# A third pair of k-tiles with seven products in the key and value blocks of a cross-attention

## The chip, the cores and the metric

The kernel runs on one core of a Trainium2 chip. The metric is device time in microseconds (us) of one execution, taken as the median over several runs; lower is better. The engines are named as the profile names them: PE is TensorE's matmuls, PEld its weight loads, DVE is VectorE, ACT is ScalarE, POOL is GpSimd, and SP issues the transfers (DMAs).

## The reference

One layer of a streaming encoder, 256 tokens of 2048 channels, in f32. Each part adds to the residual x: half a SwiGLU feed-forward, a mixer (pooling beside gated linear attention), a cross-attention to 256 memory tokens, and half a second SwiGLU; a final norm ends it. The part that the change touches is this one:

```python
def mem_cross_attention(h, mem_h, w_q, w_kv, w_o):
    q = (h @ w_q).reshape(b, s, XATTN_HEADS, XATTN_HEAD_DIM)
    kv = (mem_h @ w_kv).reshape(b, mem_h.shape[1], 2, XATTN_HEADS, XATTN_HEAD_DIM)
    k, v = kv[:, :, 0], kv[:, :, 1]
    logits = jnp.einsum('bshd,bmhd->bhsm', q, k).astype(jnp.float32) * (XATTN_HEAD_DIM ** -0.5)
    p = jax.nn.softmax(logits, axis=-1).astype(v.dtype)
    o = jnp.einsum('bhsm,bmhd->bshd', p, v).reshape(b, s, D_MODEL)
    return o @ w_o
```

There are 4 heads of 512 channels. `mem_h @ w_kv` is a product of 256 x 2048 by 2048 x 4096.

## The kernel before

**Products in three parts.** TensorE works on a format that holds fewer bits than f32, so every operand is kept as a high part (a rounded copy, written by ScalarE) and a low part (what is left, written by VectorE). A product is three matmuls: high by high, activation high by weight low, activation low by weight high (`products`, line 351). `xs` holds the activations of the current part, 16 k-tiles of 128 channels, and `ys` those of the next.

**Units and blocks.** Weights come in units of 1 MB: two k-tiles (a pair, numbered 0 to 7) by 1024 columns. A block of columns is `block_s` (line 487): eight units, taken in the order of pairs that the caller gives. Each unit is computed in one of two ways.
- Whole (`unit_p`): 2 k-tiles x 2 halves of the tokens x 2 halves of the columns, 8 products, 24 matmuls, all on line 356. Its weights are split into `wh` (ScalarE, line 273) and `wl` (VectorE, line 274).
- Seven (`unit_s` and `seven`, line 480): a Strassen-Winograd scheme, 7 products P1 to P7 on sums of operands, 21 matmuls. Its weights need three sums into a tile `T` (VectorE, line 457, three instructions), the split of the raw quarters into `xh` and `xl` (lines 273 and 274), and that of the sums into `wh` and `wl` (lines 460 and 461). The activations need sums too, once for each pair and for all blocks that share them (`Sums.make`, lines 418 to 430, and the splits of lines 279 and 280), kept in the tile `ye`. P1, P2, P3 use `xh` and `xl`; P7, P5, P6, P4 use `wh` and `wl`.

**Accumulators.** PSUM holds four tiles of two banks. A block keeps two of them from its first unit on for the sums P2, P4 and P3 and the whole products; from its first unit of seven on (`open_parts`) it keeps two more, for P1 and P6 and for P7 and P5, until `combine` (lines 547 to 552: one copy on ScalarE, three sums on VectorE) has read them behind the last unit of seven. Two joins (line 562) end the block. Everything else that TensorE writes (transposes, logits, values) takes tiles out of the same four.

**Order of the work.** `Stream` (line 34) lists units and, between them, operations that come due after a given number of units. The loads run three units ahead of the splits, on the SP queue, and the splits two units ahead of the matmuls. Within these bounds a planner of the framework sets the order of the instructions on each engine when the program is built; each engine then works in that order, and waits where it must.

**The stage.** The query product runs first (two blocks). Then come four blocks, with `xs` holding the memory tokens: keys of heads 0 and 1, values of heads 0 and 1, keys of heads 2 and 3, values of heads 2 and 3 (lines 1348 to 1359). Behind a block of keys, its result is transposed (`turn_K`, line 752), due one unit into the following block of values, the logits of both heads are due after two units (`logits`, line 1291, which also holds the softmax, lines 1297 to 1307), and the transposes of the probabilities after three (`probs`, line 1313). Behind a block of values, `ev_V` splits V into high and low (lines 279 and 280), and `values` (line 1330) is due one unit into the next block. In this stage, `KV_HOMES` lends the tiles of the units of seven other buffers: `T` takes turns with the results of `combine` on two buffers "sg", and `xh` and `xl` share two buffers "att".

Before the change, pairs 0 and 4 are computed by seven products, in one order for all four blocks: 1, 5, 2, 0, 3, 6, 4, 7. So the units of seven stand at places 3 and 6, counted from 0.

## Time and profile before

| | |
|---|---|
| median of 3 runs | 2085.72 us (2085.29 to 2086.19) |
| span of the profiled execution | 2085.1 us |
| TensorE busy / weight loads / VectorE / ScalarE | 99% / 83% / 87% / 55% |
| granted TensorE clock, mean | 0.998 |
| the stretch from 1110 to 1328 us (the four blocks) | PE 218.0, PEld 184.7, DVE 168.6, ACT 106.6 us |

The page gives the span of the profiled execution, from its first to its last instruction; it gives no other time for that execution. The times of the runs lie 0.2 to 1.1 us above it.

A line of the order of time reads: start in us, length, engine, line, operation, out<-in, shapes, how many instructions the row merges; in brackets the idle time before it and what ended it. The chain is the work that ended last, followed back from the end, as start, length, engine, tile, line, count. A busy matmul is modelled 0.39 us long while the next one starts much earlier, so the cost of a matmul is read from start to start. Lines of code behind 1260 stand one line lower in the changed kernel.

### The profile page before, as it was taken

The page shows a single profiled execution, that of the slowest core. Times are in us where ns is not written, and L with a number is a line of the kernel's source. Part 1 is how long each engine was busy: PE and PEld are TensorE (multiplying, and loading weights), DVE is VectorE, ACT ScalarE, POOL GpSimd, SP SyncE. Part 2 cuts the span into 40 slices and gives each one's busy share as a digit, 9 for nine tenths or more (in the row PEclk, how much of TensorE's full clock was granted, in tenths as well). Part 3 has the DMA queues.
Part 4 walks back from the last instruction along what each step waited for, and adds up shares of the span by engine and source line. Part 5 has one row for each costly group of instructions (what it writes and reads, how often), then busy time and mean ns, then how long its engine had stood idle before and what let it go on. Part 6 is the DMA issues. An engine that isn't in the chain of part 4 may idle for free.

```text
span 2085.1 us, 24238 instructions
## 1 busy us (share of the span) xinstructions
PE 2071.5 (99%) x9660; PEld 1727.2 (83%) x9660; DVE 1820.8 (87%) x1670; ACT 1137.5 (55%) x1128; POOL 13.1 (1%) x41
## 2 busy tenths in 40 slices
PE   9999999999999999999999999999999999999998
PEld 7888888888888888888888888888888888888886
DVE  6999899989998677579789777879998999989997
ACT  7555455554555545455755444556554556545554
POOL 0000000000000000000000000000000000000001
PEclk9999999999999999999999999999999999999999
DMA  7656766566656755457655455666576665676664
GB/s 263 201 189 235 242 220 204 187 229 232 225 197 234 238 177 182 162 182 269 225 186 188 162 182 179 205 223 203 181 242 213 236 209 190 223 241 223 204 223 159
DMA packets 131321, 435.94 MB, mean 209 GB/s; under 512 B 9860, under 2 KB 13544, under 8 KB 130824
## 3 DMA queue, kind: packets, MB, share of 16 engines
q1 hardware_dynamic: 131176, 434.38, 61.4%
q8 instruction: 76, 1.25, 0.2%
q14 instruction: 37, 0.30, 0.0%
q10 hardware_dynamic: 32, 0.01, 0.0%
HBM read 417.58 MB, written 16.78 MB: 208 GB/s over the span
## 4 chain that ended last, share of the span: by engine, by line
PE 96%; DVE 2%; issue 1%; ACT 0%; DMA 0%; SPq 0%; DVEq 0%
PE pt L356 57%; PE pt L480 26%; PE pa L341 6%; PE pb L356 2%; PE ph L752 1%; PE pl L1291 1%; PE pv L1330 1%; PE px L763 1%; DVE wl L461 0%; DVE T L457 0%; DVE xl L274 0%; DVE wl L274 0%; DMA x<-in_x 0%; PE pp L984 0%; PE pe L356 0%
## 5 line engine op out<-in xcount | busy, mean ns | idle before, releaser
L274 DVE TENSOR_TENSOR wl<-raw,wh 128x2048 fp32r<-128x2048 f32 (+2 forms) x264 | 591.4, 2247 | 131.1 <-ACT wh L273 130.4
L356 PE MATMUL pt<-wh,xs 128*128 128x512 f32 x2128 | 681.8, 390 | 0.0
L273 ACT CAST wh<-raw 128x2048 fp32r<-128x2048 f32 (+2 forms) x264 | 495.4, 1880 | 284.4 <-PE pt L356 128.1
L356 PEld LDWEIGHTS pt<-wh,xs 128*128 128x128 f32 x2128 | 398.2, 188 | 81.7 <-ACT wh L273 0.4
L356 PE MATMUL pt<-wh,ys 128*128 128x512 f32 x1472 | 464.7, 390 | 0.0
L460 ACT CAST wh<-T 128x1024 fp32r<-128x1024 f32 x236 | 248.0, 1054 | 380.5 <-DVE T L457 370.0
L356 PE MATMUL pt<-wl,xs 128*128 128x512 f32 x1064 | 415.5, 391 | 0.0
L356 PEld LDWEIGHTS pt<-wh,ys 128*128 128x128 f32 x1472 | 275.9, 188 | 56.9
L356 PE MATMUL pt<-wl,ys 128*128 128x512 f32 x736 | 286.3, 389 | 0.0
L461 DVE TENSOR_TENSOR wl<-T,wh 128x2048 fp32r<-128x2048 f32 x118 | 269.5, 2284 | 0.7
L356 PEld LDWEIGHTS pt<-wl,xs 128*128 128x128 f32 x1064 | 199.8, 188 | 41.1
L274 DVE TENSOR_TENSOR xl<-raw,xh 128x1536 fp32r<-128x1536 f32 x118 | 206.7, 1752 | 19.2 <-ACT xh L273 19.2
L273 ACT CAST xh<-raw 128x1536 fp32r<-128x1536 f32 x118 | 174.6, 1480 | 41.4 <-PE pt L480 29.2
L457 DVE TENSOR_TENSOR T<-T,raw 128x512 f32<-128x512 f32 x236 | 162.8, 690 | 6.2
L356 PEld LDWEIGHTS pt<-wl,ys 128*128 128x128 f32 x736 | 138.2, 188 | 28.6
L457 DVE TENSOR_TENSOR T<-raw 128x1024 f32<-128x1024 f32 x118 | 143.8, 1219 | 0.5
L480 PE MATMUL pt<-wh,xs 128*128 128x512 f32 x364 | 141.8, 389 | 0.0
L480 PE MATMUL pt<-xh,xs 128*128 128x512 f32 x364 | 136.6, 391 | 0.1
L341 PE MATMUL pa<-xs,wh 128*128 128x512 f32 x384 | 135.6, 397 | 0.0
L480 PE MATMUL pt<-wh,xe 128*128 128x512 f32 x320 | 124.5, 389 | 0.0
L341 PE MATMUL pa<-xs,wl 128*128 128x256 f32 x384 | 106.8, 282 | 0.0
L341 PEld LDWEIGHTS pa<-xs,wh 128*128 128x128 f32 x384 | 71.7, 188 | 16.4 <-issue 0.3
(244 smaller groups left out, 2215.6 us busy)
## 6 DMA issues: line engine op xcount, KB each, us to landing
raw<-in_ffn_w_down SPq DMA_DIRECT2D x88, 1024.0 KB, 5.5
raw<-in_ffn_w_up SPq DMA_DIRECT2D x80, 1024.0 KB, 5.0
raw<-in_ffn_w_gate SPq DMA_DIRECT2D x77, 1024.0 KB, 5.1
raw<-in_w_in SPq DMA_DIRECT2D x32, 1024.0 KB, 5.2
raw<-in_xattn_w_kv SPq DMA_DIRECT2D x32, 1024.0 KB, 5.0
raw<-in_w_out SPq DMA_DIRECT2D x16, 1024.0 KB, 5.6
raw<-in_xattn_w_q SPq DMA_DIRECT2D x16, 1024.0 KB, 5.6
raw<-in_xattn_w_o SPq DMA_DIRECT2D x16, 1024.0 KB, 5.9
```

The source lines that it names most:

```text
L273: in_turn("scalar", lambda: nc.scalar.copy(hi, src))
L274: in_turn("vector", lambda: nc.vector.tensor_tensor(out=lo, in0=src, in1=f32(hi), op=ALU.subtract))
L341: nc.tensor.matmul(o, w, x, start=k == 0 and i == 0, stop=last and i == 1)
L356: nc.tensor.matmul(ps, a, w, start=first and i == 0, stop=last and i == 2)
L457: in_turn("vector", lambda: nc.vector.tensor_tensor(out=o, in0=a, in1=b, op=ALU.add))
L460: in_turn("scalar", lambda: nc.scalar.copy(th[:, c], t[:, c]))
L461: in_turn("vector", lambda: nc.vector.tensor_tensor(out=tl, in0=t, in1=f32(th), op=ALU.subtract))
L480: nc.tensor.matmul(banks[n], x, w, start=n in fresh and j == 0, stop=n in ends and j == 2)
L752: nc.tensor.transpose(v[:, i, h * P : (h + 1) * P], g[:, h, i * P : (i + 1) * P], ident)
L763: nc.tensor.transpose(v[:, j, h * P : (h + 1) * P], x[:, h, j * P : (j + 1) * P], ident)
L1291: nc.tensor.matmul(ps[:, t, :M], ys[:, 4 * h + d, a, tok], xa["K", h][:, d, b, :], start=i == 0, stop=i == 11,)
L1330: nc.tensor.matmul(ps[:, d, :S], xa["V", h][:, m, a, col], xa["PT", h][:, m, b, :], start=i == 0, stop=i == 5,)
```

## The change

A third pair, number 2, is computed by seven products in all four blocks. Its sums of activations are made in addition, due after the third unit, and `ye` holds three pairs instead of two. The order of the pairs changes: the first block of keys takes 1, 5, 3, 0, 6, 2, 4, 7 (seven at places 3, 5 and 6), and the other three blocks take 1, 2, 5, 0, 3, 4, 6, 7 (seven at places 1, 3 and 5).

```diff
-    kv_sums, KV_ORDER = Sums("ye", xs, (0, 4), True, 2), (1, 5, 2, 0, 3, 6, 4, 7)
+    kv_sums = Sums("ye", xs, (0, 2, 4), True, 3)
+    KV_ORDER = ((1, 5, 3, 0, 6, 2, 4, 7), (1, 2, 5, 0, 3, 4, 6, 7))
...
-    for g, after in zip(kv_sums.pairs, (0, 2)):
+    for g, after in zip(kv_sums.pairs, (0, 2, 3)):
         st.op(lambda g=g: among_weights(lambda: kv_sums.make(g)), after)
     for b in range(2):
-        block_s(wwide(w_kv, b * 2 * NB), xs, kv_sums, KV_ORDER, lambda j, c, b=b: held.__setitem__(
+        block_s(wwide(w_kv, b * 2 * NB), xs, kv_sums, KV_ORDER[b], lambda j, c, b=b: held.__setitem__(
             ("K", 2 * b + j), c))
...
-        block_s(wwide(w_kv, D + b * 2 * NB), xs, kv_sums, KV_ORDER, ev_V(b))
+        block_s(wwide(w_kv, D + b * 2 * NB), xs, kv_sums, KV_ORDER[1], ev_V(b))
```

## The prediction

> **What bounds the kernel now.** First the page: its first line, the busy line and the chain that ended last.

> ```profile
> span 2085.1 us, 24238 instructions
> PE 2071.5 (99%) x9660; PEld 1727.2 (83%) x9660; DVE 1820.8 (87%) x1670; ACT 1137.5 (55%) x1128; POOL 13.1 (1%) x41
> PE 96%; DVE 2%; issue 1%; ACT 0%; DMA 0%; SPq 0%; DVEq 0%
> ```

> The time is TensorE's, and VectorE stands right behind it. The second view is the stretches view of the four blocks of keys and values, which I call K1, V1, K2, V2 in the order in which they run. Its columns are PE, weight load, VectorE and ScalarE busy.

> ```profile
> 1110.00:1328.00 218.00, 218.00 (x1077) 184.68 (x1076) 168.55 (x155) 106.61 (x102) 0.00 (x0) 1.00 0.52 177
> ```

> TensorE never rests here, and VectorE has 49.5 us to spare, in pieces. Third, the chain in order of time (start, length, what):

> ```profile
> 1060.25 5.44 PE pt L356 x24
> 1065.69 0.47 PE pt L480 x2
> 1066.18 1.49 ACT xh L273
> 1067.70 1.77 DVE xl L274
> 1069.51 2.11 PE pt L480 x8
> 1117.33 10.43 PE pt L356 x46
> 1143.40 1.75 PE ph L752 x16
> 1153.69 5.63 PE pl L1291 x47
> 1163.67 0.44 PE pt L1313 x4
> ```

> 46 matmuls take 10.43 us, so a matmul costs 0.2267 us, start to start. A whole unit (24) is 5.44 us and a unit of seven products (21) is 4.76 us. The four rows from 1065.69 show what a wait ahead of a unit of seven looks like; it lies in the query block, ahead of the change.

> **The change, part by part.** *Products.* Each of the four blocks drops one of eight products of one pair: 3 matmuls, 12 in all, 12 x 0.2267 = 2.72 us off TensorE. The built program confirms it: 84 matmuls more on line 480 and 96 fewer on line 356. Nothing hides TensorE's work here, so these 2.72 us (0.13%) are the whole gain, and the floor is 2083.0.

> *VectorE.* I need the steps from one start to the next, and take them from VectorE's order of time in K1.

> ```profile
> 1095.63 0.68 DVE L418 TENSOR_TENSOR j<-xs 128x512 f32<-128x512 f32 x1
> 1097.54 2.29 DVE L274 TENSOR_TENSOR wl<-raw,wh 128x2048 fp32r<-128x2048 f32 x1
> 1099.74 1.22 DVE L457 TENSOR_TENSOR T<-raw 128x1024 f32<-128x1024 f32 x1
> 1100.88 0.28 DVE L280 TENSOR_TENSOR xs<-j,xs 128x128 fp32r<-128x128 f32 x1
> 1101.55 0.68 DVE L457 TENSOR_TENSOR T<-T,raw 128x512 f32<-128x512 f32 x1
> ...
> 1112.04 0.28 DVE L425 TENSOR_TENSOR j<-j 128x128 f32<-128x128 f32 x1
> 1113.21 4.48 DVE L274 TENSOR_TENSOR wl<-raw,wh 128x2048 fp32r<-128x2048 f32 x2
> 1117.62 1.22 DVE L457 TENSOR_TENSOR T<-raw 128x1024 f32<-128x1024 f32 x1
> ...
> 1119.43 1.41 DVE L457 TENSOR_TENSOR T<-T,raw 128x512 f32<-128x512 f32 x2
> 1120.75 1.75 DVE L274 TENSOR_TENSOR xl<-raw,xh 128x1536 fp32r<-128x1536 f32 x1
> 1122.42 2.28 DVE L461 TENSOR_TENSOR wl<-T,wh 128x2048 fp32r<-128x2048 f32 x1
> 1124.62 2.29 DVE L274 TENSOR_TENSOR wl<-raw,wh 128x2048 fp32r<-128x2048 f32 x1
> 1129.79 2.29 DVE L274 TENSOR_TENSOR wl<-raw,wh 128x2048 fp32r<-128x2048 f32 x1 [2.88 <-ACT wh L273]
> 1132.50 0.69 DVE L548 TENSOR_TENSOR sg<-pt,sg 128x512 f32<-128x512 f32 x1 [0.42 <-ACT sg L547]
> ...
> 1135.09 2.28 DVE L274 TENSOR_TENSOR wl<-raw,wh 128x2048 fp32r<-128x2048 f32 x1
> 1137.29 2.35 DVE L562 TENSOR_TENSOR sg<-pt,sg 128x1024 f32<-128x1024 f32 x2
> ```

> A whole unit costs VectorE 2.20 (1097.54 to 1099.74). A unit of seven costs 1.14 + 1.32 + 1.67 + 2.20 = 6.33, and 6.45 where no other instruction fills its dependent steps. The sums of one pair cost 1.91 (1095.63 to 1097.54) + 0.67 (1100.88 to 1101.55) = 2.6; combine 2.59 (1132.50 to 1135.09); the two joins 2.27. So the change adds 4 x 4.2 + 2.6 = 19.4 us to VectorE for 2.7 us off TensorE. By total it fits into the 49.5 us; what counts is where.

> *Place A, K1 into V1.* Units of seven stand at places 3, 5 and 6 of K1 (3 and 6 before), and at place 1 of V1 (3 before). In the built order VectorE runs from 1112.04 (unchanged until there): the rest of the sums of pair 4, 1.84; a whole unit, 2.20; the new sums of pair 2, 2.59; two units of seven, 12.90; two whole ones, 4.40; combine 2.59; V1's unit of seven, 6.45; the joins 2.27; the weights of V1's third unit, 2.29. That is 37.5 without a rest: they are ready at 1149.6. TensorE, from the end of K1's first unit of seven (1117.2), has 123 matmuls and the 16 transposes of line 752 until it asks for them: 27.88 + 1.75, so it would be there at 1146.8. It waits 2.8. Before, the row at 1129.79 shows the rest of 2.88 that VectorE had in this very stretch. Bounds: 0, if handovers were better than these steps; 3.9, if every small wait on the way also cost a restart. I take 2.8, with a restart 2.9.

> *Place B, the shared buffers.* In these blocks the tiles xh and xl share the two buffers "att", so ScalarE can fill the next xh only when TensorE has done P1 of the unit of seven before. In V1, K2 and V2 the new order puts P1, P6, P7 and P5 of the first unit late, straight ahead of the second unit of seven, since the accumulators for them are still taken. That is what happened in the query block:

> ```profile
> 1068.93 0.39 PE L480 MATMUL pt<-wh,xs 128*128 128x512 f32 x1
> 1069.51 0.50 PE L480 MATMUL pt<-xl,xs 128*128 128x512 f32 x1 [0.19 <-DVE xl L274]
> 1069.85 0.39 PE L480 MATMUL pt<-xh,xs 128*128 128x512 f32 x1
> ...
> 1071.46 0.47 PE L356 MATMUL pt<-wh,xs 128*128 128x512 f32 x1
> 1071.94 0.50 PE L480 MATMUL pt<-wl,xs 128*128 128x512 f32 x1
> 1072.28 0.40 PE L480 MATMUL pt<-wh,xs 128*128 128x512 f32 x1
> ```

> Against steps of 0.2267 the two breaks cost 0.35 + 0.11 + 0.25 + 0.11 = 0.8 us. After P1 the new order leaves 9 matmuls and 4 that need only the high parts: 13 x 0.2267 = 2.95 against 1.49 + 1.77 and two handovers, so again a break of some 0.4, then one on wl. Three blocks: 2.4 (bounds 0.6, where ScalarE is quicker, and 4).

> *Place C, the softmax of heads 0 and 1.* With the accumulators opened at V1's second unit, no bank is left for the logits until V1's combine; in the built order they stand in V1's last unit, where V1's order had them in its third before. The transposes of head 1's probabilities stand on TensorE four transposes behind V1's last matmul. But on VectorE that head's normalization stands behind the second join, which needs that last matmul, and behind the low part of V.

> ```profile
> 1162.58 0.17 DVE L1305 RECIPROCAL sm<-sm 128x2 f32<-128x2 f32 x1 [1.15 <-ACT P L1301]
> 1162.78 0.62 DVE L1307 TENSOR_SCALAR P<-P,sm 128x256 f32<-128x256 f32 x2
> ...
> 1194.04 2.35 DVE L280 TENSOR_TENSOR V<-sg,V 128x1024 fp32r<-128x1024 f32 x2
> ```

> From VectorE's order of time: join 1.2, V 1.2, reciprocal 0.2 and the first half of P 0.31, with 0.2 for the matmul's own end and the handovers, are 3.1; four transposes (the last row of the chain above) cover 0.44. TensorE, in order, waits 2.7 with K2's first units behind it, and 0.1 to restart. Bounds 2.2 and 3.2: both ends hang on the same matmul, so nothing earlier moves them. For heads 2 and 3 the built order has the normalization ahead of the second join; it is ready about 1 us before TensorE asks: 0 (bounds 0 and 2.8).

> *The rest, at nothing.* ScalarE gets 4 x (1.48 + 2.1 - 1.9) = 6.7 us and idles for 111 in the stretch. The 32 weight loads are the same in other order on SP, three units ahead; raw buffers are given back up to 3 us later, against 5.0 us from issue to landing in units of 5 us, so the next one still lands in time. The tile of sums grows by half and moves nothing. The values of V1 now stand together in K2's second to fourth unit, with 0.2 of waits on accumulators, inside B's bound. Those of V2 fall into the output block; its weights stay some microseconds ahead.

> **The sum.** -2.7 + 2.9 + 2.4 + 2.8 = +5.4 us. It is made on the execution of 2085.1 us span; the median of the runs, 2085.72, lies 0.6 above that span, and what lies around the span does not change: 2085.7 + 5.4 = 2091.1.

> [...]

> **The rivals.**
> 1. *TensorE is not held up.* VectorE's rest over the stretch (49.5 us) takes up all 19.4, and the time is 2083.0, not slower. For it: not one wait of TensorE stands in this stretch now. It decides at one point: V1's third weights would have to be ready by 1146.8 and head 1's probabilities within four transposes. Against it: the sum of rows at A, and C's order.
> 2. *Only one of A and C is real.* 2091.1 - 2.8 = 2088.3. For it: 2.8 of 37 is a small difference of large sums.
> 3. *More places of the same kind.* The second softmax waits too (2.8), or VectorE stays behind through K2: 2094 to 2095.
> 4. *VectorE bounds the whole stretch.* Its added 19.4 us would all show: 2085.7 + 19.4 = 2105. Against it: its 77% there.

> That the change does something else than it says is ruled out by the built order's count of products.

> **How the numbers follow.** My forecast 0.62 (2089 to 2093.5), rival 1 0.07, rival 2 0.17, rival 3 0.12, rival 4 0.02. About 0.2% (4.2 us) is what a measurement of this kernel can tell from no change. Faster by that would need 2081.5, beyond the floor: 0.01. Rivals 1 and 2 and the lower edge of the forecast lie within it: 0.26. The rest is slower: 0.73. The range leaves out rival 1, rival 4 and the ends: 2087 to 2095.

> **What would show it.** In the new profile TensorE's waits should name VectorE at K1's weights (lines 274 and 461) and at the transposes of line 1314, once, of about 2.7 us, ahead of heads 0 and 1 alone; VectorE should stand without a rest for 37 us from K1's start; breaks of 0.3 to 0.4 us stand in front of the second unit of seven in V1, K2 and V2. The prediction falls if the stretch shows no rest of TensorE, or if VectorE gets through K1 with time to spare.

## The result and the profile after

The changed kernel takes 2092.81 us (2091.82 to 2093.22) against 2085.95 us for the kernel before, measured beside it: 6.86 us more, a ratio of 1.0032 with a 95% interval of 1.0022 to 1.0042. So it is slower, and by more than the 0.2% that a measurement can tell from no change. The profiled execution spans 2090.8 us.

The page's first line, the busy line and the chain that ended last:

```profile
span 2090.8 us, 24247 instructions
PE 2074.5 (99%) x9648; PEld 1725.8 (83%) x9648; DVE 1839.5 (88%) x1693; ACT 1145.6 (55%) x1138; POOL 13.1 (1%) x41
PE 94%; DVE 4%; issue 1%; ACT 1%; DMA 0%; SPq 0%; DVEq 0%; ACTq 0%
```

TensorE has 12 matmuls fewer, and VectorE now holds 4% of the chain that ended last, in place of 2%. The stretch of the four blocks, and the waits of TensorE in it (in total, times, longest); the kernel before had not one wait there:

```profile
1110.00:1333.00 223.00, 218.10 (x1054) 180.74 (x1054) 185.52 (x176) 113.11 (x111) 0.00 (x0) 0.99 0.50 170
```

```profile
PE pt L1314 <- DVE P L1308: 2.6, 1, 2.6
PE pt L480 <- DVE xl L274: 1.4, 3, 1.0
PE pt L356 <- DVE wl L274: 0.7, 1, 0.7
```

VectorE is busy for 185.5 of 223 us, so it still has 37 us to spare; TensorE rests for 4.9 us all the same, in five waits of three kinds, each time for VectorE. A granted clock of 0.99 instead of 1.00 is the fourth thing to look at. TensorE's order of time shows all of it. These are rows at which a step from start to start is longer than it should be; of the second units of seven in V1, K2 and V2 only V1's is shown, since the three look alike:

```profile
1126.51 0.39 PE L480 MATMUL pt<-wh,xs 128*128 128x512 f32 x1
1127.91 0.50 PE L480 MATMUL pt<-xl,xs 128*128 128x512 f32 x1 [1.02 <-DVE xl L274]
...
1145.44 1.91 PE L752 MATMUL ph<-ident,sg 128*128 128x128 f32 x16
1148.03 0.50 PE L356 MATMUL pt<-wl,xs 128*128 128x512 f32 x1 [0.67 <-DVE wl L274]
...
1156.57 0.39 PE L480 MATMUL pt<-wh,xs 128*128 128x512 f32 x1
1157.14 0.50 PE L480 MATMUL pt<-xl,xs 128*128 128x512 f32 x1 [0.19 <-DVE xl L274]
...
1188.41 0.60 PE L1314 MATMUL pt<-ident,P 128*128 128x128 f32 x4
1191.57 0.44 PE L1314 MATMUL pt<-ident,P 128*128 128x128 f32 x1 [2.57 <-DVE P L1308]
1191.67 0.77 PE L356 MATMUL pt<-wh,xs 128*128 128x512 f32 x1
1192.24 0.63 PE L356 MATMUL pt<-wl,xs 128*128 128x512 f32 x1
1192.67 1.05 PE L356 MATMUL pt<-wh,xs 128*128 128x512 f32 x2
1193.52 0.63 PE L356 MATMUL pt<-wl,xs 128*128 128x512 f32 x1
1193.95 1.03 PE L356 MATMUL pt<-wh,xs 128*128 128x512 f32 x2
1194.80 0.42 PE L356 MATMUL pt<-wl,xs 128*128 128x512 f32 x1
```

From such rows, with 0.2267 us for a matmul and 0.11 for a transpose taken off each step, the losses are:

| place | forecast us | measured us |
|---|---|---|
| products, 12 matmuls fewer | -2.72 | -2.72 |
| A: breaks in the two neighbouring units of seven in K1 | | 1.85 |
| A: V1's third weights (row at 1148.03) | 2.9 in all | 0.93 |
| B: second unit of seven in V1, K2, V2 | 2.4 | 0.79 + 0.99 + 0.79 = 2.57 |
| C: head 1's probabilities (row at 1191.57) | 2.8 | 2.72 |
| slow matmuls right behind C | not foreseen | 1.54 |
| second softmax (heads 2 and 3) | 0 | 0 |
| sum | +5.4 | +6.9 |

The sum of the pieces, 6.9, meets the difference of the medians, 6.86, closer than the measurement allows (the interval of the ratio is 4.6 to 8.8 us), so that part of the agreement is luck. In the two traces, from the transposes of line 752 at the start of K1 to the next ones behind V2 it takes 409.88 us (1098.49 to 1508.37) against 402.42 before (1100.17 to 1502.59), 7.5 us more, which is the pieces and some 0.6 us in steps too small to list. The spans differ by 5.7 us only, because the execution after had come to this part 1.7 us earlier, through work that the change does not touch.

The row "slow matmuls" comes from the last rows of the fence: from 1192.24 on, three matmuls take 1.28 us (1192.24 to 1193.52) instead of 0.68. The stretches view before, in and behind these rows names the reason in its third number from the right, the granted clock:

```profile
1185.00:1188.40 3.40, 3.40 (x16) 2.77 (x15) 2.07 (x6) 2.86 (x7) 0.00 (x0) 1.00 0.30 122
1191.60:1195.00 3.40, 3.40 (x9) 2.72 (x10) 3.40 (x4) 1.01 (x2) 0.00 (x0) 0.53 0.05 6
1195.00:1198.00 3.00, 3.00 (x16) 2.44 (x16) 2.36 (x4) 0.00 (x0) 0.00 (x0) 1.00 0.86 307
```

The clock is 1.00 ahead of the wait, 0.53 for 3.4 us behind it, and 1.00 again. (0.53 is a mean: the clock stands at 0.50 from 1191.41 to 1194.82, and the second stretch shown begins and ends 0.2 us later.)

### The profile page after: what moved, and what is told of

Same layout as the page of the kernel before. It is cut to its first block, busy times and chain, and to the rows that moved or that the text cites. A ratio compares the mean times of both kernels' runs of the same rounds, so it can differ in the third digit from the quotient of the medians.

```text
span 2090.8 us, 24247 instructions
## 1 busy us (share of the span) xinstructions
PE 2074.5 (99%) x9648; PEld 1725.8 (83%) x9648; DVE 1839.5 (88%) x1693; ACT 1145.6 (55%) x1138; POOL 13.1 (1%) x41
## 4 chain that ended last, share of the span: by engine, by line
PE 94%; DVE 4%; issue 1%; ACT 1%; DMA 0%; SPq 0%; DVEq 0%; ACTq 0%
PE pt L356 55%; PE pt L480 26%; PE pa L341 6%; PE pb L356 2%; PE ph L752 1%; DVE xl L274 1%; DVE wl L274 1%; DVE T L457 1%; DVE wl L461 1%; PE pl L1292 1%; PE pv L1331 1%; PE px L763 1%; ACT xh L273 0%; PE pp L984 0%; PE pe L356 0%
## 5 line engine op out<-in xcount | busy, mean ns | idle before, releaser
L274 DVE TENSOR_TENSOR wl<-raw,wh 128x2048 fp32r<-128x2048 f32 (+2 forms) x260 | 582.5, 2247 | 118.8 <-ACT wh L273 118.3
L356 PE MATMUL pt<-wh,xs 128*128 128x512 f32 x2064 | 664.7, 391 | 0.0
L273 ACT CAST wh<-raw 128x2048 fp32r<-128x2048 f32 (+2 forms) x260 | 487.6, 1879 | 256.6 <-PE pt L356 110.0
L460 ACT CAST wh<-T 128x1024 fp32r<-128x1024 f32 x244 | 256.5, 1054 | 383.7 <-DVE T L457 380.0
L356 PE MATMUL pt<-wh,ys 128*128 128x512 f32 x1472 | 464.8, 390 | 0.0
L356 PEld LDWEIGHTS pt<-wh,xs 128*128 128x128 f32 x2064 | 387.4, 188 | 80.1 <-ACT wh L273 0.9
L356 PE MATMUL pt<-wl,xs 128*128 128x512 f32 x1032 | 403.8, 391 | 0.7 <-DVE wl L274 0.7
L356 PEld LDWEIGHTS pt<-wh,ys 128*128 128x128 f32 x1472 | 275.9, 188 | 56.9
L356 PE MATMUL pt<-wl,ys 128*128 128x512 f32 x736 | 286.4, 389 | 0.0
L461 DVE TENSOR_TENSOR wl<-T,wh 128x2048 fp32r<-128x2048 f32 x122 | 278.7, 2285 | 0.7
L356 PEld LDWEIGHTS pt<-wl,xs 128*128 128x128 f32 x1032 | 194.3, 188 | 40.9 <-DVE wl L274 0.9
L274 DVE TENSOR_TENSOR xl<-raw,xh 128x1536 fp32r<-128x1536 f32 x122 | 213.7, 1752 | 13.2 <-ACT xh L273 13.2
L273 ACT CAST xh<-raw 128x1536 fp32r<-128x1536 f32 x122 | 180.5, 1480 | 42.2 <-PE pt L480 25.8
L457 DVE TENSOR_TENSOR T<-T,raw 128x512 f32<-128x512 f32 x244 | 168.5, 691 | 6.5
L356 PEld LDWEIGHTS pt<-wl,ys 128*128 128x128 f32 x736 | 138.2, 188 | 28.5
L457 DVE TENSOR_TENSOR T<-raw 128x1024 f32<-128x1024 f32 x122 | 148.8, 1219 | 0.5
L480 PE MATMUL pt<-wh,xs 128*128 128x512 f32 x380 | 148.0, 389 | 0.0
L480 PE MATMUL pt<-xh,xs 128*128 128x512 f32 x380 | 143.0, 391 | 0.1
L480 PE MATMUL pt<-wh,xe 128*128 128x512 f32 x320 | 124.5, 389 | 0.0
```

The lines of the kernel that those rows point to most:

```text
L273: in_turn("scalar", lambda: nc.scalar.copy(hi, src))
L274: in_turn("vector", lambda: nc.vector.tensor_tensor(out=lo, in0=src, in1=f32(hi), op=ALU.subtract))
L356: nc.tensor.matmul(ps, a, w, start=first and i == 0, stop=last and i == 2)
L457: in_turn("vector", lambda: nc.vector.tensor_tensor(out=o, in0=a, in1=b, op=ALU.add))
L460: in_turn("scalar", lambda: nc.scalar.copy(th[:, c], t[:, c]))
L461: in_turn("vector", lambda: nc.vector.tensor_tensor(out=tl, in0=t, in1=f32(th), op=ALU.subtract))
```

## The experiments

The orders of units are given to the four blocks one by one in these kernels: `KV_ORDER` holds K1, K2, V1, V2, each with its order and its pairs of seven, and the two calls of `block_s` take them from there. Only the orders are shown in the diffs. In the kernels where a block computes pair 2 whole, "K1 alone", "V1 as before" and "K1 as before" with its shifted twin, those whole units read the activations of pair 2 that its sums have overwritten. These four kernels therefore don't give the layer's result; the work and its order are what counts there. A median over few runs carries some 2 us of uncertainty, as the intervals show, so single places are read in the traces, and the medians are used for sums.

### V's split behind the normalization (place C by itself)

```diff
-            split(V[:, :, 0, :], V[:, :, 1, :], c)
+            with tc.issue_after(xa["normal"].ins):
+                split(V[:, :, 0, :], V[:, :, 1, :], c)
...
-            nc.vector.tensor_scalar_mul(pr[:, t, :], pr[:, t, :], sm[:, t : t + 1])
+            xa["normal"] = nc.vector.tensor_scalar_mul(pr[:, t, :], pr[:, t, :], sm[:, t : t + 1])
```

> The changed kernel, with one order turned round: the split of V (high and low parts) is issued behind the normalization of the probabilities, so that on VectorE the low part of V no longer stands ahead of head 1's probabilities. Nothing else moves. My theory: the wait at the transposes of head 1 falls from 2.6 us by the 1.2 of that instruction to about 1.4, and the half-rate matmuls behind it (1.5 us lost, granted clock 0.53) go with it if they come from the length of TensorE's rest: 2.7 less, about 2090.1. If the half rate comes from what follows the wait and not from its length: 1.2 less, 2091.6. Rival (the price is VectorE's total work, wherever it stands): nothing changes, 2092.8.

Measured: 2090.42 us, ratio 1.0021 (1.0012 to 1.0031). VectorE's order of time in the changed kernel, and then in this one:

```profile
1188.61 1.23 DVE L562 TENSOR_TENSOR sg<-pt,sg 128x1024 f32<-128x1024 f32 x1 [0.48 <-PE pt L356]
1189.75 1.22 DVE L280 TENSOR_TENSOR V<-sg,V 128x1024 fp32r<-128x1024 f32 x1
1190.88 0.16 DVE L1306 RECIPROCAL sm<-sm 128x2 f32<-128x2 f32 x1
1191.08 0.62 DVE L1308 TENSOR_SCALAR P<-P,sm 128x256 f32<-128x256 f32 x2
```

```profile
1189.41 1.22 DVE L562 TENSOR_TENSOR sg<-pt,sg 128x1024 f32<-128x1024 f32 x1 [0.48 <-PE pt L356]
1190.55 0.15 DVE L1307 RECIPROCAL sm<-sm 128x2 f32<-128x2 f32 x1
1190.74 0.62 DVE L1309 TENSOR_SCALAR P<-P,sm 128x256 f32<-128x256 f32 x2
1191.28 1.22 DVE L280 TENSOR_TENSOR V<-sg,V 128x1024 fp32r<-128x1024 f32 x1
```

The second join comes first in both, and V's low part stands behind the normalization in the second. TensorE's wait there falls from 2.57 to 1.43 us, the other waits stay, and the clock is 1.00 in the 3.4 us behind it. By the trace that is 1.1 us of the wait and the 1.5 of the slow matmuls, by the medians 2.4; place C is VectorE's order behind V1's last matmul, as predicted. What is left, 1.4, is the join, the reciprocal and half of P.

### No two units of seven close together

```diff
-    KV_ORDER = ((1, 5, 3, 0, 6, 2, 4, 7), (1, 2, 5, 0, 3, 4, 6, 7))
+    KV_ORDER = (((1, 5, 0, 3, 2, 6, 4, 7), (0, 2, 4)), ((1, 2, 5, 3, 0, 6, 4, 7), (0, 2, 4)),
+                ((1, 2, 5, 3, 0, 6, 4, 7), (0, 2, 4)), ((1, 2, 5, 3, 0, 6, 4, 7), (0, 2, 4)))
```

with V's split behind the normalization as above.

> All three pairs of products in all four blocks, but no two units of seven next to each other (K1's order 1,5,0,3,2,6,4,7, that of V1, K2 and V2 1,2,5,3,0,6,4,7), and V's split issued behind the normalization of the probabilities. Theory (the loss is in the places where units of seven stand close, and in the softmax's place): the floor of 2083.0, the softmax's wait of 1.5 that moving the split alone left, and at most 0.8 in K1, where one whole unit lies between: 2084.5 to 2086, no slower than before the change. Rival (VectorE has too much work in this stretch, wherever it stands): it falls behind elsewhere, and the time stays at the 2090.4 that moving the split alone gave.

Measured: 2100.77 us, ratio 1.0073 (1.0058 to 1.0088), the slowest of all. Both expectations fell. TensorE's order of time:

```profile
1122.33 0.50 PE L356 MATMUL pt<-wl,xs 128*128 128x512 f32 x1 [1.49 <-DVE wl L274]
...
1181.42 5.91 PE L1294 MATMUL pl<-K,ys 128*128 128x256 f32 x48
1193.41 1.36 PE L1316 MATMUL pt<-ident,P 128*128 128x128 f32 x5 [6.08 <-DVE P L1310]
...
1287.80 5.91 PE L1294 MATMUL pl<-K,ys 128*128 128x256 f32 x48
1297.85 1.36 PE L1316 MATMUL pt<-ident,P 128*128 128x128 f32 x5 [4.14 <-DVE P L1310]
```

The breaks in front of units of seven are nearly gone, but place A is not: K1 now waits 1.49 us for the weights of a whole unit (the row at 1122.33), which on VectorE stand behind the sums of activations of a pair, and V1's third weights come 0.45 us late. With the restarts that is 2.5 us, against 2.8 in the changed kernel. And the last unit of seven of V1 and V2 stands one place later, so their accumulators come free later: the logits of two heads now stand behind V1's and V2's last unit, with the transposes right behind them. All of the softmax lies open, for 6.1 and 4.1 us, and slow matmuls follow both (granted 0.50 and 0.51). So the place of the logits, which follows from when an accumulator comes free, is worth more than all other places of this change together.

### K2 with two whole units between its first and second unit of seven (place B)

```diff
-    KV_ORDER = ((1, 5, 3, 0, 6, 2, 4, 7), (1, 2, 5, 0, 3, 4, 6, 7))
+    KV_ORDER = (((1, 5, 3, 0, 6, 2, 4, 7), (0, 2, 4)), ((1, 2, 5, 3, 0, 6, 4, 7), (0, 2, 4)),
+                ((1, 2, 5, 0, 3, 4, 6, 7), (0, 2, 4)), ((1, 2, 5, 0, 3, 4, 6, 7), (0, 2, 4)))
```

> The changed kernel with two whole units in place of one between K2's first and second unit of seven (K2's order 1,2,5,3,0,6,4,7); all else stays. Theory (B: ScalarE may fill the next xh only behind P1 of the unit of seven before, and P1 comes late): with a whole unit more in between, the break of 0.8 to 1.0 us in front of K2's second unit of seven goes, those of V1 and V2 stay, and the time is 2092.8 - 0.9 = 2091.9. Rival (VectorE is late in K2 from V1's joins, wherever the units stand): the break only moves, 2092.8. In either case the wait of 2.6 us at head 1's transposes and the slow matmuls behind it stay.

Measured: 2091.78 us, ratio 1.0028 (1.0017 to 1.0038). The theory's 2091.9 and the rival's 2092.8 both lie inside this interval; the trace tells them apart. K2's breaks shrink from 0.99 to 0.33 us; those of V1 and V2 and the wait of C stay. The break in front of P1 (0.27 + 0.10) is gone, and with it one of 0.27 behind the values, in front of K2's first unit of seven. The one in front of the first matmul with `wl` (0.23 and 0.10) is not: VectorE still starts on `xl` only when ScalarE has filled `xh`, after a rest of its own.

```profile
1219.86 1.76 DVE L274 TENSOR_TENSOR xl<-raw,xh 128x1536 fp32r<-128x1536 f32 x1 [5.22 <-ACT xh L273]
1221.76 2.29 DVE L461 TENSOR_TENSOR wl<-T,wh 128x2048 fp32r<-128x2048 f32 x1
```

So B is not VectorE's load: it rests for 5.2 us ahead of this very row.

### The units of seven of V1 and V2 late, as in K1

```diff
-    KV_ORDER = ((1, 5, 3, 0, 6, 2, 4, 7), (1, 2, 5, 0, 3, 4, 6, 7))
+    KV_ORDER = (((1, 5, 3, 0, 6, 2, 4, 7), (0, 2, 4)), ((1, 2, 5, 0, 3, 4, 6, 7), (0, 2, 4)),
+                ((1, 5, 3, 0, 6, 2, 4, 7), (0, 2, 4)), ((1, 5, 3, 0, 6, 2, 4, 7), (0, 2, 4)))
```

> As changed, with the same number of products, but both blocks of values take K1's order (1, 5, 3, 0, 6, 2, 4, 7), so that the accumulators for the products of seven open at the fourth unit, behind logits and probabilities. My theory: the softmax wait and the breaks of V1 and V2 go (4.3 + 0.9 + 1.6), two units of seven that now stand next to each other in V1 and V2 cost some 0.6 each: about 2087.2. Rival (VectorE's total is the same): 2092.8.

Measured: 2095.27 us, ratio 1.0044 (1.0029 to 1.0059). The theory's number fell, though C and V1's wait for its third weights are gone as it said; the rival's 2092.8 lies within the interval. In V1 and V2 two units of seven now stand next to each other, and each such pair costs 2.4 us. VectorE's rows and then TensorE's, in V1:

```profile
1173.62 1.76 DVE L274 TENSOR_TENSOR xl<-raw,xh 128x1536 fp32r<-128x1536 f32 x1 [1.59 <-ACT xh L273]
1175.52 2.29 DVE L461 TENSOR_TENSOR wl<-T,wh 128x2048 fp32r<-128x2048 f32 x1
...
1180.32 1.75 DVE L274 TENSOR_TENSOR xl<-raw,xh 128x1536 fp32r<-128x1536 f32 x1
```

```profile
1180.74 0.39 PE L480 MATMUL pt<-wh,xs 128*128 128x512 f32 x1
1182.12 0.50 PE L480 MATMUL pt<-xl,xs 128*128 128x512 f32 x1 [0.99 <-DVE xl L274]
```

VectorE had rested 1.59 us ahead of the first unit's `xl`, and is late for the second's all the same: from one `xl` to the next it needs 6.7 us (1173.62 to 1180.32), and TensorE 4.8 for a unit of seven. K2 pays too: its values wait, 2.6 us in all, the most of it for ScalarE's part of V, by the chain that the next experiment shows. By the traces the stretch from 1100.13 to 1510.81 is 0.8 us longer here than the same stretch of the changed kernel (409.88); the rest of the 2.5 us between the medians lies outside it and is not explained.

### V1 as before the change

```diff
-    KV_ORDER = ((1, 5, 3, 0, 6, 2, 4, 7), (1, 2, 5, 0, 3, 4, 6, 7))
+    KV_ORDER = (((1, 5, 3, 0, 6, 2, 4, 7), (0, 2, 4)), ((1, 2, 5, 0, 3, 4, 6, 7), (0, 2, 4)),
+                ((1, 5, 2, 0, 3, 6, 4, 7), (0, 4)), ((1, 2, 5, 0, 3, 4, 6, 7), (0, 2, 4)))
```

> The change in K1, K2 and V2; V1 alone as before (pairs 0 and 4, order 1, 5, 2, 0, 3, 6, 4, 7). My theory: V1 gave back 4.3 (softmax with the slow matmuls behind it), 0.8 (shared buffers) and 0.9 (the end of VectorE's run without a rest) for 0.7 of products, so this is 5.3 below the changed kernel: about 2087.5. Rival (VectorE's total, 19.4 us for 9.6 us lost, spread over four blocks): a quarter less, 1.7 below: 2091.1.

Measured: 2090.01 us, ratio 1.0020 (1.0011 to 1.0029), between the two numbers. TensorE's waits:

```profile
PE pt L480 <- DVE xl L274: 1.2, 2, 1.0
PE pv L1332 <- ACT V L279: 1.0, 1, 1.0
PE pt L356 <- DVE wl L274: 0.4, 1, 0.4
PE pv L1332 <- DVE ys L280: 0.2, 1, 0.2
```

C and V1's part of A are gone. In their place the values in K2 wait. VectorE's order of time shows what they are behind:

```profile
1188.56 1.22 DVE L457 TENSOR_TENSOR T<-raw 128x1024 f32<-128x1024 f32 x1
...
1192.81 2.28 DVE L461 TENSOR_TENSOR wl<-T,wh 128x2048 fp32r<-128x2048 f32 x1
1195.01 2.35 DVE L562 TENSOR_TENSOR sg<-pt,sg 128x1024 f32<-128x1024 f32 x2
```

K2 has its first unit of seven at place 1, and the 6.5 us that it takes on VectorE stand ahead of V1's joins; ScalarE's part of V follows the joins, and the values follow that. It costs 2.2 us (1.14 + 0.66 + 0.39), two fifths of the 5.3 that the theory had V1 give back, and nearly all that the measured time lies above the theory's.

### The third pair in K1 alone, and K1 as before

```diff
-    KV_ORDER = ((1, 5, 3, 0, 6, 2, 4, 7), (1, 2, 5, 0, 3, 4, 6, 7))
+    KV_ORDER = (((1, 5, 3, 0, 6, 2, 4, 7), (0, 2, 4)), ((1, 5, 2, 0, 3, 6, 4, 7), (0, 4)),
+                ((1, 5, 2, 0, 3, 6, 4, 7), (0, 4)), ((1, 5, 2, 0, 3, 6, 4, 7), (0, 4)))
```

> The third pair in K1 alone, in its new order; the other three blocks as before. My theory: VectorE's run without a rest remains in K1 and costs 1.9 there, 0.7 is saved: 1.2 above the kernel before, about 2087.1; the other blocks show no wait. Rival (a quarter of VectorE's added work): 1.7 above, 2087.6; this run tells the two apart by where the waits stand, not by the time.

Measured: 2087.44 us, ratio 1.0007 (0.9997 to 1.0016). The trace has K1's breaks, 1.83 us in all, the largest 1.15 in front of the second of the neighbouring units, and nothing in the other blocks.

```diff
-    KV_ORDER = ((1, 5, 3, 0, 6, 2, 4, 7), (1, 2, 5, 0, 3, 4, 6, 7))
+    KV_ORDER = (((1, 5, 2, 0, 3, 6, 4, 7), (0, 4)), ((1, 2, 5, 0, 3, 4, 6, 7), (0, 2, 4)),
+                ((1, 2, 5, 0, 3, 4, 6, 7), (0, 2, 4)), ((1, 2, 5, 0, 3, 4, 6, 7), (0, 2, 4)))
```

> K1 has its units, its order and its two units of seven as before the change; V1, K2 and V2 are as changed (the third sums are still made in K1). Theory (A comes of the run of VectorE through K1 and into V1): K1's breaks of 1.85 us go and the third weights of V1 come in time (0.93 less), for 0.68 us of products more: 2092.8 - 2.8 + 0.7 = 2090.7, with VectorE resting in K1. Rival (each place by itself, as K1 alone gave +1.5 us): 2092.8 - 1.5 = 2091.3, with V1's wait for its third weights still there.

Measured: 2090.30 us, ratio 1.0024 (1.0014 to 1.0033). TensorE's waits:

```profile
PE pt L1315 <- DVE P L1309: 2.6, 1, 2.6
PE pt L480 <- DVE ys L280: 1.0, 1, 1.0
PE pt L480 <- DVE xl L274: 0.6, 3, 0.2
```

K1's breaks are gone, and V1's third weights come in time, as the theory said: with one unit of seven less in K1, VectorE is busy for 43.3 of the 50 us from 1110 to 1160, against 46.6 in the changed kernel. The time, 0.4 under the theory's, is no proof of it by itself, since two other things moved. A new wait of 1.14 us stands at 1109, for VectorE's part of the turned queries. And behind the unchanged wait of 2.6 us the slow matmuls are missing. That was not expected, and the next runs went after it.

### What brings the slow matmuls

Three edits. The first adds two multiplications by one ahead of head 1's normalization, on top of the later V split; the second adds transposes at the start of the program (8, 16 or 24), so that all else comes later; the third puts the eight transposes into the kernel with K1 as before.

```diff
+        for _ in range(2 if h == 1 else 0):
+            nc.vector.tensor_scalar_mul(pr[:, 0, :], pr[:, 0, :], 1.0)
...
-                nc.tensor.transpose(
-                    v[:, j, h * P : (h + 1) * P], x_cols((k + j) * P, P)[:, h], ident
-                )
+                for _ in range(3 if c > 3 and j == h == 0 else 1):
+                    nc.tensor.transpose(
+                        v[:, j, h * P : (h + 1) * P], x_cols((k + j) * P, P)[:, h], ident
+                    )
```

> The changed kernel with V's split issued behind the normalization, and two more multiplications by one of half of head 1's probabilities ahead of their normalization: TensorE's wait there goes from 1.4 to some 2.0 us. If the low clock follows a wait of 2.6 but not one of 1.4 us: where it decides is open; with the clock full behind 2.0 us the time is 2090.4 + 0.6 = 2091.0, with it at half 2092.5. Rival (it wasn't the wait's length that brought the low clock, but that V's split ran beside it): the clock stays full in any case, 2091.0.

> The changed kernel with eight transposes more (some 0.9 us) among the first units of the program, so that everything behind them stands later by as much; the stretch itself keeps its order up to the late transposes. Theory (TensorE's clock is set from one fixed stretch of some 3.4 us to the next; a wait of 2.6 us lowers it only if it fills most of one such stretch): the wait stays at 2.6 us, but where it lies in such a stretch moves, so the slow matmuls behind it may last shorter or be gone: between 2091.3 + 0.9 = 2092.2 (gone) and 2093.7. Rival (the wait's length alone lowers the clock): the same 1.5 us of slow matmuls, 2093.7, here and in the two kernels that follow.

> The same with sixteen transposes (some 1.8 us). Theory: of the three shifts at least one shows the wait of 2.6 us with no slow matmul behind it, as in the kernel without K1's change; this one lies between 2093.1 (none) and 2094.6 (as many as without a shift). Rival: 2094.6.

> The same with twenty-four transposes (some 2.6 us). Theory: between 2093.9 and 2095.4. Rival: 2095.4.

> The kernel with K1 as before the change, whose profile showed the wait of 2.6 us at the softmax with no slow matmul behind it, with the eight transposes more at the program's start (they moved the stretch by 1.2 us in the changed kernel). Theory (whether the clock falls hangs on where the wait lies in time, not on this kernel's order): the same wait, now with slow matmuls behind it as in the changed kernel and its three shifts, 2090.3 + 1.2 + 1.5 = 2093.0. Rival (with K1's order as before, something keeps the clock up behind such a wait): full clock again, 2091.5.

Measured, with TensorE's wait at the transposes of head 1:

| kernel | us | wait us | most rest in one stretch of 3.41 us | granted clock in the next stretch | lost to it us |
|---|---|---|---|---|---|
| changed kernel | 2092.81 | 2.57 | 2.40 | 0.50 | 1.54 |
| V's split later | 2090.42 | 1.43 | 1.43 | 1.00 | 0 |
| two multiplications more | 2093.09 | 3.16 | 2.50 | 0.50 | 1.60 |
| K2 spaced | 2091.78 | 2.57 | 2.57 | 0.50 | 1.69 |
| 8 transposes more | 2093.91 | 2.56 | 2.22 | 0.50 | 1.48 |
| 16 transposes more | 2096.03 | 2.56 | 2.56 | 0.50 | 1.56 |
| 24 transposes more | 2094.75 | 2.57 | 2.57 | 0.50 | 1.57 |
| K1 as before | 2090.30 | 2.56 | 1.51 | 1.00 | 0 |
| K1 as before, 8 transposes more | 2091.79 | 2.57 | 1.33 | 1.00 | 0 |

The multiplications made the wait longer than meant, 3.16 us and not 2.0, since V's low part slipped in between the two halves of P. The 8, 16 and 24 transposes moved the wait by 1.2, 4.1 and 2.3 us (the 16 cost more than their own time at the program's start), and all three kernels kept the slow matmuls, so the expectation that one of them would lose them fell. The shift in the kernel with K1 as before was 0.6 us only, and its clock stayed full, which was the rival's number (2091.5). So a wait of 2.6 us was followed by 3.4 us at half the clock in five profiles and by none in two, both with K1 as before; one of 1.4 us was followed by none.

The traces show what goes with it. In the changed kernel the clock's changes lie on a grid of 3.413 us: it falls at 1191.41, rises at 1194.82 and falls again at the program's end, at 2085.70, and from 1194.82 to 2085.70 are 261 times 3.413 us. In the trace of the kernel before, the record of the clock begins at 5.84 and the clock falls at 2077.73, 607 times 3.413 us later; from the 1191.41 of the changed kernel to 2077.73 it is 259.66 times, so the grid lies elsewhere in the two traces. The clock of a stretch went with TensorE's rest in the stretch before it. These are two neighbouring stretches in the kernel with 16 transposes more, and two in the last kernel of the table (its grid is known from the clock's fall at 2084.57, at the program's end); the first number behind the length is TensorE's busy time:

```profile
1192.87:1196.28 3.41, 0.84 (x6) 0.59 (x5) 3.38 (x6) 3.41 (x7) 0.00 (x0) 1.00 0.00 0
1196.28:1199.69 3.41, 3.41 (x10) 2.67 (x9) 3.41 (x4) 0.40 (x1) 0.00 (x0) 0.50 0.22 36
```

```profile
1186.87:1190.28 3.41, 2.08 (x12) 1.51 (x10) 2.89 (x7) 2.92 (x6) 0.00 (x0) 1.00 0.00 0
1190.28:1193.69 3.41, 2.17 (x10) 1.86 (x11) 3.37 (x5) 2.27 (x3) 0.00 (x0) 1.00 0.00 0
```

In the first the wait lies whole in one stretch, and the next one runs at half the clock. In the second a border of the grid divides it into 1.33 and 1.24 us, and the clock stays full; in the kernel with K1 as before it is divided into 1.51 and 1.06. No stretch of the two traces of before and after speaks against this: of 1215 at the full clock, the clock fell behind three, with 2.40 us of rest (at the wait of C), 2.26 and 3.41 (both at the program's end), and behind none of the others, in which TensorE rested for 1.26 us at most. So these runs agree with the theory of the fixed stretch, though the number that it gave for the shifts fell: that all three put more than 2.2 us of the wait into one stretch, and that both kernels with K1 as before did not, is by the theory where the grid happened to lie. K1's order is not needed to explain it. The loss may then come and go between executions of one kernel; that is an estimate, as only one execution of each kernel was traced. The runs of K1 as before neither bear it out nor speak against it: the slowest, 2091.89 us, has a mean granted clock of 0.997, the other eight have 0.998 or 0.999, but not in the order of their times (0.998 at 2089.85, 0.999 at 2090.25 and 2090.30).

## Why the prediction was right, and where it was not

The forecast, 2091.1, is 1.7 us under the measured 2092.81, and inside the range. The direction, the engine that is waited for and, but for half of A, the places came out as said. Without the slow matmuls the pieces add up to 5.35 us, against the forecast 5.4; so close a sum is partly luck, as the errors of its terms (0.1 to 0.2 each) cancel.

- *Products.* 12 matmuls fewer, as counted. Nothing else came off.
- *Place A.* The sum was right, 2.78 measured for 2.9, but it stands at two places, and the step "TensorE ... would be there at 1146.8. It waits 2.8" is only half of it. VectorE did run without a rest, from 1110.4 to 1152.7, and needed 37.6 us to the end of V1's third weights (1110.36 to 1147.97), as the forecast's 37.5 had it. These weights were the last thing to be late (0.93; gone with K1 as before). But 1.85 had been paid in K1 already, in the two neighbouring units of seven, the most of it (1.4) at the second. Such a break comes wherever two of them are neighbours: it is there with the third pair in K1 alone, and in V1 where VectorE had rested before. But neighbours are not the whole cause, since with whole units between them K1 still lost 1.8, ahead of a whole unit's weights; what both have is VectorE's work without a rest, with the sums of a third pair in it. Since TensorE works in order, what it waits for early it no longer waits for later, and the sum over VectorE's run hid the mistake.
- *Place B.* 2.57 for 2.4, at the three places named. Spacing the units in K2 took away the part in front of P1 and left that in front of `wl`, so the reason given (P1 comes too close to the next unit of seven) holds for half of K2's 0.72; its other 0.27 stood behind the values, within the bound that the forecast gave for them.
- *Place C.* The wait was 2.72 for the forecast 2.7, by the very chain that was given: join, V's low part, reciprocal, half of P. Putting V's split behind took 1.1 off. With V1's first unit of seven back at place 3 the logits start at 1156.1 and 1155.7 (the blocks of values late, V1 as before) in place of 1178.3, and the wait is gone, which bears out the step from the place of that unit to the place of the logits. The mis-sized term is "0.1 to restart": behind the wait TensorE's granted clock was 0.50 for 3.4 us, which cost 1.54. This one term is nearly the whole of the 1.7 us that the forecast lacks. No wait of such length stood ahead of matmuls in the profile of before, so no row there showed this cost; the bound "2.2 and 3.2" took the restart for a fixed small cost. Whether it came went, in these traces, with where the wait fell on the clock's grid (2.40 us of it in one stretch here, 1.51 with K1 as before), which the forecast could not know.
- *The second softmax.* No wait, as the forecast had it.
- *The rivals.* The first (TensorE is not held up) is out by the waits. The second (only one of A and C real) is out: both are. The third named the second softmax, or VectorE behind through K2, and neither came; its number, 2094 to 2095, was missed too, though the slow matmuls moved the time towards it. The fourth (VectorE bounds the whole stretch) is out by VectorE's 37 us of rest.

No order tried here was faster than the kernel before; the nearest, the third pair in K1 alone, can't be told from it (1.0007, 0.9997 to 1.0016). With a floor of 0.13% under the old time there was little to win.

## What to carry to other kernels

Where an engine is full and its feeder has a sixth of its time to spare, cost a change by the longest run of the feeder's work between two of its rests, in the order in which it was built, and look for each place where its lead is short: two heavy units next to each other lose time even behind a rest, and moving them apart may only move the loss. Before units are moved, follow what their place does to accumulators and to the small chains (logits, softmax, transposes) that wait for one: here these were worth more than the products saved. And count a wait of TensorE like those here (2.6 us and more) at its length plus the 1.5 to 1.7 us that the half clock cost behind six of the eight in the table and did not behind the other two.
